# One 512-column matmul for both token parts in the FFN, z and merge-gate products, and one pool of four PSUM banks for products and transposes

## Chip, cores and metric

The kernel runs on one core of one Trainium2 chip. The metric is the device time of one execution in microseconds, as the median of several runs. TensorE is called PE, VectorE DVE, ScalarE ACT, GpSimd POOL, and SyncE, which issues the loads, SP.

## The reference

The input is 256 tokens of width 1024, in fp32. A first block runs four branches on one normalised input and merges them through gates. A second block follows, two layers deep, in which each layer is an FFN, a mixer (MLA in layer 0, NSA in layer 1) and another FFN. Cut to what the change touches:

```python
# first block
h = _rmsnorm(x, norm_pre)
(dn_qkv, dn_z, dn_b, dn_a, gm_uv, gm_z, sw_q, sw_k, sw_v, sw_z,
 xm_q, xm_z, gate_logits) = _split_cols(h @ w_in)
y_a = _deltanet_branch(dn_qkv, dn_z, dn_b, dn_a, ...)   # convolution, L2 norms, chunked delta rule
y_b = _spatial_gating_branch(gm_uv, gm_z, ...)
y_c = _sliding_window_branch(sw_q, sw_k, sw_v, sw_z, sinks)   # attention * silu(z)
y_m = _memory_branch(xm_q, xm_z, mem_kv)                      # attention * silu(z)
proj = einsum("btnc,ncd->btnd", stack([y_a, y_b, y_c, y_m]), w_up)
merged = sum(sigmoid(gate_logits) * proj, axis=2)
x = x + _rmsnorm(merged @ w_out, norm_post)
# second block, for i in (0, 1)
h = h + 0.5 * swiglu(rmsnorm(h, ffn_norm_a[i]), ...)
h = h + (mla_mixer if i == 0 else nsa_mixer)(rmsnorm(h, mix_norm[i]), ...)
h = h + 0.5 * swiglu(rmsnorm(h, ffn_norm_b[i]), ...)
def swiglu(x, w_gate, w_up, w_down):                # hidden width 2816
    return (silu(x @ w_gate) * (x @ w_up)) @ w_down
```

## The kernel before

**Numbers in two parts.** A large product is computed in three matmuls. Weights and activations are each split into a high part, which is the value cast to fp32r, and a low part, which is the remainder. `mm3` (L226 to L232) adds high x high (L227), then the two mixed products (L229 and L231), into one PSUM region. The weights stream in: `unit` (L192) loads up to 1 MB into `raw` (two buffers, SP's queue), ACT casts it to `wh` in two halves (L210), and DVE subtracts to get `wl` (L211), into a ring of four buffers. `transposes` (L328) turns activations on PE, with ACT writing the high part (L356, `xTh`) and DVE the low one (L357, `xTl`).

**Two forms of product.** In `Product` (L240) and `ts` the activations are stationary and 512 weight columns move. In `ws` (L289) a 128x128 block of weights is stationary and the 256 tokens move. One call of `mm3` in `ws` is thus three matmuls of 256 columns, called a triple here. Two row blocks of 256 columns share a 512-column bank, and an evacuation function given by the caller reads the full bank. `ws` is used for z of two branches (`z_ws`, L505), the convolution inputs (`convolve`), two query products of the first block, the merge gates (L1010), the up-projections of the merge, the queries of NSA, and gate and up of every FFN chunk but the first (`hidden`, L1080). `silu2` (L404) is a tanh on ACT (L413) and a multiply on DVE (L414), both from the bank.

**Banks.** PSUM has eight banks. `acc` is a pool of two (L111), `tr`, for transposes, another of two (L114). The other four go to the mixer of the moment (`mm`, `po` and so on) or to the four accumulators `d` of an FFN's down product.

**What sets the order.** The program is written as a stream of large products, with small work dripped into it: after each matmul `drip` takes the next entry of `pending` (a transpose, or a pause) or the next step of a generator in `beside` (deltanet, sliding attention, memory attention). The framework then reorders instructions within each engine by readiness and priority. A tile of a pool is given out in the order in which the program asks for it. So an instruction that needs a new tile of one tag can't be moved ahead of an earlier request of the same tag that is still waiting, while requests of two tags are free of each other.

**Places named below.** First, the deltanet start: `convolve` evacuates a product to `xpad` (L580), runs four taps (ACT, then DVE L586), silu, squares (L597), and `norms` sums the squares with one-column matmuls into a `tr` bank (L603), before the scores of deltanet (L689) and its levels (L721, L730). Second, the tail of sliding attention: scores (L894), softmax on DVE and ACT, transposes of the probabilities `pr` (L335), copies `pT` on DVE (L450), values (L925). Third, the ends of MLA and NSA: the output product (`AddOut`, banks `mm`, `wo`) is added to `res` (L1162), `Normed` squares it on ACT (L312), POOL makes 1/rms (L317, L318), DVE scales (L384, `xn`), PE transposes, and the next FFN begins with `first_hidden`, whose first half of tokens has been transposed earlier.

Of the kernel before, what the change touches and what calls it, by code (L numbers as in the profile page):

```python
# [10 lines left out]
F32 = mybir.dt.float32  # L11
# [6 lines left out]
P = 128  # L18
# [75 lines left out]
def two_blocks_kernel(ctx: ExitStack, tc: tile.TileContext, a, cst_dram, cst2_dram, out):  # L94
# [14 lines left out]
            DEBUG.append("dbg_" + name)  # L109

    def acc():  # L111
        return psum.tile([P, 512], F32, name="acc", bufs=2)

    def tr():  # L114
        return psum.tile([P, 512], F32, name="tr", bufs=2)

    def mixer_banks(stack, *tags):

# [3 lines left out]
    class Turns:  # L122


        def __init__(self, first, second):
            self.banks, self.n = [first, second], 0
# [10 lines left out]
    def drip():  # L137
        for _ in range(pace[0]):
            step()
# [86 lines left out]
    def mm3(ps, ah, al, bh, bl, start, stop):  # L226
# [4 lines left out]
        pe.matmul(ps, al, bh, start=False, stop=stop)  # L231
        drip()  # L232

    def block(x, k, t):

        nb = x[0][0].shape[1]
        h, l = x[k // nb]
        return h[:, k % nb, t * P:(t + 1) * P], l[:, k % nb, t * P:(t + 1) * P]
# [50 lines left out]
    def ws(x, nk, W, r0, c0, n, evac):  # L289

        w = 512 if nk <= 4 else 256
        for j0 in range(0, n, w):
            h, l = unit(W, r0, nk, c0 + j0, w)
            for j1 in range(0, w, 256):
                pv = acc().rearrange("p (j t) -> p j t", j=2)
                for j in range(2):
                    js = slice(j1 + j * P, j1 + (j + 1) * P)
                    for k in range(nk):
                        xh, xl = (v[:, k % v.shape[1], :] for v in x[k // x[0][0].shape[1]])
                        mm3(pv[:, j, :], h[:, k, js], l[:, k, js], xh, xl, k == 0, k == nk - 1)  # L300
                evac((j0 + j1) // P, 2, pv)

    def rstd(ss, eps, n=1):
        r = small.tile([P, n], F32, name=f"rstd{n}")
        gp.tensor_scalar(r, ss, eps, None, op0=OP.add)
        gp.tensor_tensor(r, r, nhalf[:, :n], op=OP.pow)
        return r
# [53 lines left out]
            flush()  # L361

    def xpair():
        h = per.tile([P, 8, T], F32R, name="xTh", bufs=1)
        l = per.tile([P, 8, T], F32R, name="xTl", bufs=1)
        return [(h, l)]

    def ypair():
        h = per.tile([P, 4, T], F32R, name="yTh", bufs=2)
# [34 lines left out]
    def silu2(dst, ps, ph):  # L404

        th = ph.tile([P, 512], F32, name="th", bufs=2)
        n = 1
        for s in ps.shape[1:]:
            n *= s
        thv = th[:, :n]  # L410
        if len(ps.shape) == 3:
            thv = thv.rearrange("p (a b) -> p a b", a=ps.shape[1])
        sc.activation(thv, ps, AF.Tanh, scale=0.5)  # L413
        ve.scalar_tensor_tensor(dst, thv, 1.0, ps, op0=OP.add, op1=OP.mult)  # L414
# [54 lines left out]
    def first(nxt):  # L469
# [36 lines left out]
        def z_ws(name, c0):  # L506

            z = ph.tile([P, 4, T], F32, name="y_" + name)
            y[name] = z
            ws(xT, 8, w_in, 0, c0, 512, lambda j0, w, pv: silu2(z[:, j0:j0 + w, :], pv, ph))  # L510


        bl = ph.tile([P, 2, 8], F32)
# [482 lines left out]
        for at, (br, name) in enumerate([(1, "b"), (2, "c"), (0, "a"), (3, "m")]):  # L996
            if name == "c":
                finish(sliding)
            if name == "m":
                finish(memory)  # L1000
            yT = [ypair()]
            for t in range(2):
                if name in "ab":
                    split_T(y[name][:, t, :], 4, yT, t)
                else:
                    ks_ = slice(2 * t, 2 * t + 2)
                    split(y[name][:, ks_, :], [v[:, ks_, :] for v in yT[0]])
            for n in range(2):
                gate = pg.tile([P, 4, T], F32, name="gate", bufs=1)
                ws(xT, 8, w_in, 0, 5896 + br * D + n * 512, 512,  # L1010
                   lambda j0, w, pv, gate=gate: sc.activation(gate[:, j0:j0 + w, :], pv, AF.Tanh, scale=0.5))
                if at == 3:
                    moT.append(ypair())

                def ev(j0, w, pv, n=n, gate=gate, at=at):
                    g, m = gate[:, j0:j0 + w, :], merged[:, 4 * n + j0:4 * n + j0 + w, :]
                    if at == 0:
                        ve.scalar_tensor_tensor(m, g, 1.0, pv, op0=OP.add, op1=OP.mult)
                    else:
                        ve.scalar_tensor_tensor(g, g, 1.0, pv, op0=OP.add, op1=OP.mult)  # L1020
                        ve.tensor_add(m, m, g)
                    if at == 3:
                        split(m, [v[:, j0:j0 + w, :] for v in moT[n]])

                ws(yT, 4, a["w_up"][0, br], 0, n * 512, 512, ev)
# [27 lines left out]
    def ffn(i, which, xn, nxt, aside=None):  # L1053
        pace[0] = 1
        wg, wu, wd = (a[f"ffn_{which}_w_{s}_2"][i] for s in ("gate", "up", "down"))
        nxt.load()
        fx = ExitStack()
        pf = fx.enter_context(tc.tile_pool(name=f"ffn{which}{i}", bufs=2))
        pd = fx.enter_context(tc.tile_pool(name="down", bufs=1, space=bass.MemoryType.PSUM))
        dacc = {(t, m): pd.tile([P, 512], F32, name=f"d{t}{m}") for t in range(2) for m in range(2)}  # L1060
        xT = xn.x
        chunks = [(0, 512), (512, 512), (1024, 512), (1536, 512), (2048, 256), (2304, 512)]

        def first_hidden(c0, n):

            sg = {}

            def ev_g(t, g, p):
                sg[t] = pf.tile([P, 512], F32, name="sg", bufs=4)
                silu2(sg[t], p, pf)  # L1070

            def ev_u(t, g, p):
                ve.tensor_mul(sg[t], sg[t], p)

            pg = Product(xT, 8, wg, 0, c0, n, ev_g)
            pu = Product(xT, 8, wu, 0, c0, n, ev_u)
            in_turns([(pg, 0), (pg, 1), (pu, 0), (pu, 1)], lead=4)
            hT = [ypair()]
            for t in range(2):
                split_T(sg[t], n // P, hT, t, wait=LAG_HIDDEN if t == 0 else 0)  # L1080
            return hT

        def hidden(c0, n):

            hT = ypair()
            for j0 in range(0, n, 256):
                sg = pf.tile([P, 2, T], F32, name="sg", bufs=4)

                def ev_u(j, w, p, js=slice(j0 // P, j0 // P + 2), sg=sg):
                    ve.tensor_mul(sg, sg, p)  # L1090
                    sc.copy(hT[0][:, js, :], sg)
                    ve.tensor_sub(hT[1][:, js, :], sg, f32(hT[0][:, js, :]))

                ws(xT, 8, wg, 0, c0 + j0, 256, lambda j, w, p, sg=sg: silu2(sg, p, pf))
                ws(xT, 8, wu, 0, c0 + j0, 256, ev_u)
            return [hT]

        def down_units(c0, n):
            nk = n // P
            if nk == 4:  # L1100
                return {m: units(wd, c0, nk, m * 512, 512)[0] for m in range(2)}
            both, = units(wd, c0, nk, 0, D)
            return {m: [(h[:, halves[m]], l[:, halves[m]]) for h, l in both] for m in range(2)}

        def down(us, hT, t, m, first, last):
            nk = len(us[m])
            for k, (h, l) in enumerate(us[m]):
                mm3(dacc[t, m], *block(hT, k, t), h, l, first and k == 0, last and k == nk - 1)

        def add_down(t, m):  # L1110
            ve.scalar_tensor_tensor(res[:, t, halves[m]], dacc[t, m], 0.25, res[:, t, halves[m]],
                                    op0=OP.mult, op1=OP.add)

        prev = None
        for c, (c0, n) in enumerate(chunks):
            hT = hidden(c0, n) if c else first_hidden(c0, n)
            if prev is not None and c < len(chunks) - 1:
                us = down_units(*prev[:2])
                for m in range(2):
                    for t in range(2):  # L1120
                        down(us, prev[2], t, m, c == 1, False)
            elif prev is not None:
                held = (down_units(*prev[:2]), prev[2])
                for m in range(2):
                    down(*held, 0, m, False, False)
            prev = (c0, n, hT)
            if c == 1 and aside:
                aside()
        us = down_units(*prev[:2])
        for m in range(2):  # L1130
            down(us, prev[2], 0, m, False, True)
            add_down(0, m)
        nxt(0)
        for m in range(2):
            down(*held, 1, m, False, False)
        for m in range(2):
            down(us, prev[2], 1, m, False, True)
            add_down(1, m)
        nxt(1)
        fx.close()  # L1140
# [542 lines left out]
```

## Time and profile before

| | us |
|---|---|
| median of 3 runs | 1436.03 (1435.72 to 1440.63) |
| profiled execution, its own time | 1434.2 |
| its span in the profile | 1432.4 |
| PE busy | 1408.2 (98%) |
| DVE busy | 873.9 (61%) |
| ACT busy | 686.5 (48%) |
| POOL busy | 44.3 (3%) |

The profile is one execution. Its own time is 1.8 us longer than its span. "Busy" of PE is modelled, since matmuls overlap: the row of a matmul gives its start and a duration that reaches into the next one. What a matmul takes of PE's time is read from the distance between two starts. Every row gives line, engine, operation, output and input tile, shape, and in square brackets the idle time of that engine just before and what ended it.

### The profile page before, as it was taken

To read this page: it belongs to the slowest core of one execution; us is meant where nothing else is said; L and a number is where in the kernel's file an instruction comes from. 1 tells how busy PE (TensorE), PEld (TensorE's weight loads), DVE (VectorE), ACT (ScalarE), POOL (GpSimd) and SP (SyncE) were. 2 spreads that over 40 slices of the span, in tenths; PEclk is the share of its full clock that TensorE was granted. 3 is DMA by queue.
4 is the path that set the end of the run, shared out by engine and by line. 5 is a ranking of instruction groups with operands and counts; after the bars stand their busy time and mean duration, and the time that the engine had idled before them with its cause. 6 is when DMAs were issued, how large, how long until landed. Compare 5 with 4: busy or idle time off the path is not lost.

```text
span 1432.4 us, 23501 instructions
## 1 busy us (share of the span) xinstructions
PE 1408.2 (98%) x9712; PEld 1278.7 (89%) x9712; DVE 873.9 (61%) x1443; ACT 686.5 (48%) x1149; POOL 44.3 (3%) x87
## 2 busy tenths in 40 slices
PE   7999999999999999999999999999999999999998
PEld 7998989999979999887799998999898976799997
DVE  6878575565576555668565546655555676665544
ACT  6646454443354433466453435443435376554432
POOL 1002000000010000110000000000000000000000
PEclk9999999999999999999999999999999999999999
DMA  7425634555546655433567655565665620465551
GB/s 260 143 89 177 220 107 144 177 177 177 177 157 215 198 180 180 161 119 121 167 208 257 212 177 183 184 206 177 201 205 182 168 60 30 133 201 185 195 185 59
DMA packets 172543, 241.90 MB, mean 169 GB/s; under 512 B 5263, under 2 KB 121748, under 8 KB 172308
## 3 DMA queue, kind: packets, MB, share of 16 engines
q1 hardware_dynamic: 172436, 240.40, 52.3%
q8 instruction: 76, 1.25, 0.3%
q14 instruction: 31, 0.25, 0.1%
HBM read 239.31 MB, written 4.22 MB: 170 GB/s over the span
## 4 chain that ended last, share of the span: by engine, by line
PE 91%; DMA 3%; DVE 2%; ACT 2%; POOL 1%; issue 1%; SPq 0%; POOLq 0%; ACTq 0%
PE acc L231 20%; PE acc L227 20%; PE acc L229 20%; PE d L227 5%; PE d L229 5%; PE d L231 5%; PE tr L335 4%; DMA raw<-in_nsa_w_in_dram 1%; DVE wl L211 1%; ACT wh L210 1%; PE wo L1512 1%; PE mm L1512 1%; PE po L730 1%; PE po L721 1%; DMA raw<-in_ffn_b_w_up_dram 1%
## 5 line engine op out<-in xcount | busy, mean ns | idle before, releaser
L211 DVE TENSOR_TENSOR wl<-raw,wh 128x1024 fp32r<-128x1024 f32 (+5 forms) x434 | 512.5, 1198 | 330.3 <-ACT wh L210 329.6
L210 ACT CAST wh<-raw 128x1024 fp32r<-128x1024 f32 (+5 forms) x434 | 436.1, 1028 | 527.3 <-PE acc L229 278.8
L227 PE MATMUL acc<-xTh,wh 128*128 128x256 f32 x1696 | 483.3, 285 | 0.0
L229 PE MATMUL acc<-xTl,wh 128*128 128x256 f32 x1696 | 483.1, 285 | 0.0
L231 PE MATMUL acc<-xTh,wl 128*128 128x256 f32 x1696 | 482.8, 285 | 0.0
L227 PEld LDWEIGHTS acc<-xTh,wh 128*128 128x128 f32 x1696 | 325.1, 192 | 2.2 <-PE d L231 0.6
L229 PEld LDWEIGHTS acc<-xTl,wh 128*128 128x128 f32 x1696 | 325.2, 192 | 1.4 <-issue 0.3
L231 PEld LDWEIGHTS acc<-xTh,wl 128*128 128x128 f32 x1696 | 325.2, 192 | 0.7 <-issue 0.5
L227 PE MATMUL d<-wh,yTh 128*128 128x512 f32 x352 | 137.7, 391 | 0.0
L229 PE MATMUL d<-wl,yTh 128*128 128x512 f32 x352 | 137.7, 391 | 0.0
L231 PE MATMUL d<-wh,yTl 128*128 128x512 f32 x352 | 137.7, 391 | 0.0
L227 PE MATMUL acc<-wh,xTh 128*128 128x512 f32 (+4 forms) x256 | 97.6, 382 | 0.5 <-ACT xTh L356 0.5
L231 PE MATMUL acc<-wh,xTl 128*128 128x512 f32 (+4 forms) x256 | 96.2, 378 | 0.2 <-DVE xTl L357 0.2
L229 PE MATMUL acc<-wl,xTh 128*128 128x512 f32 (+4 forms) x256 | 96.2, 376 | 0.0
L231 PEld LDWEIGHTS d<-wh,yTl 128*128 128x128 f32 x352 | 66.1, 188 | 14.3
L227 PEld LDWEIGHTS d<-wh,yTh 128*128 128x128 f32 x352 | 66.2, 188 | 13.4
L229 PEld LDWEIGHTS d<-wl,yTh 128*128 128x128 f32 x352 | 66.2, 188 | 13.1
L1090 DVE TENSOR_TENSOR sg<-sg,acc 128x512 f32<-128x512 f32 x36 | 24.7, 687 | 53.3 <-PE acc L231 53.3
L231 PEld LDWEIGHTS acc<-wh,xTl 128*128 128x128 f32 x256 | 48.6, 190 | 8.9 <-DVE xTl L357 0.9
L227 PEld LDWEIGHTS acc<-wh,xTh 128*128 128x128 f32 x256 | 48.8, 191 | 8.7 <-ACT xTh L356 1.2
L229 PEld LDWEIGHTS acc<-wl,xTh 128*128 128x128 f32 x256 | 48.9, 191 | 7.5
L231 PE MATMUL acc<-yTh,wl 128*128 128x256 f32 x160 | 45.5, 284 | 0.0
(442 smaller groups left out, 1753.2 us busy)
## 6 DMA issues: line engine op xcount, KB each, us to landing
raw<-in_w_in_dram SPq DMA_DIRECT2D x37, 1024.0 KB, 5.2
raw<-in_ffn_a_w_gate_dram SPq DMA_DIRECT2D x22, 1024.0 KB, 5.3
raw<-in_ffn_a_w_up_dram SPq DMA_DIRECT2D x22, 1024.0 KB, 5.4
raw<-in_ffn_a_w_down_dram SPq DMA_DIRECT2D x22, 1024.0 KB, 5.0
raw<-in_ffn_b_w_gate_dram SPq DMA_DIRECT2D x22, 1024.0 KB, 5.4
raw<-in_ffn_b_w_up_dram SPq DMA_DIRECT2D x22, 1024.0 KB, 5.3
raw<-in_ffn_b_w_down_dram SPq DMA_DIRECT2D x22, 1024.0 KB, 5.1
raw<-in_w_up_dram SPq DMA_DIRECT2D x8, 1024.0 KB, 5.0
```

The costliest lines, as they stand in the source:

```text
L210: sc.copy(h[:, c], raw[:, c])
L211: ve.tensor_sub(l[:, c], raw[:, c], f32(h[:, c]))
L227: pe.matmul(ps, ah, bh, start=start, stop=False)
L229: pe.matmul(ps, ah, bl, start=False, stop=False)
L231: pe.matmul(ps, al, bh, start=False, stop=stop)
L335: pe.transpose(box[0][:m, b * P:(b + 1) * P], src(b), ident)
L721: pe.matmul(pv[:, h], O[:, h, :], dv[:, h], start=True, stop=True)
L730: pe.matmul(p[:, h * 64:(h + 1) * 64], Em[:, h, :], Vs[t][:, h, :], start=True, stop=True)
L1090: ve.tensor_mul(sg, sg, p)
L1512: pe.matmul(s[:, i, :], qT[half(h), h // 2, tsl], kT[br][half(h), h // 4, 0:w], start=True, stop=True)
```

## The change

A class `Pair` holds high and low part of the activations in one tile of shape 128 x 8 x 2 x 256, so that both parts of one k are adjacent. A new function `ws2` does the product of `ws` with two matmuls for each k: one of 512 columns with the high weights (both parts at once, into both halves of a bank), one of 256 columns with the low weights (into the first half). Each 128-row block has a bank of its own. The evacuation is an ACT copy of the second half to SBUF and a DVE add of the first half, and then the caller's function reads SBUF. `ws2` takes the place of `ws` for the two z products, the merge gates, and gate and up of the FFN chunks but the first. `acc` gets four banks, and `tr` becomes another name of `acc`.

```diff
     def acc():
-        return psum.tile([P, 512], F32, name="acc", bufs=2)
-
-    def tr():
-        return psum.tile([P, 512], F32, name="tr", bufs=2)
+        return psum.tile([P, 512], F32, name="acc", bufs=4)
+
+    tr = acc
...
+    class Pair:
+        def __init__(self, t):
+            self.t = t
+            self.parts = (t[:, :, 0, :], t[:, :, 1, :])
...
+        def both(self, k):
+            return self.t[:, k]
...
+    def ws2(x, nk, W, r0, c0, n, into, evac=None, scale=None):
+        w = 512 if nk <= 4 else 256
+        for j0 in range(0, n, w):
+            h, l = unit(W, r0, nk, c0 + j0, w)
+            for j1 in range(0, w, 256):
+                b = (j0 + j1) // P
+                dst = into(b)
+                for j in range(2):
+                    js = slice(j1 + j * P, j1 + (j + 1) * P)
+                    ps = acc()
+                    for k in range(nk):
+                        pair = x[k // x[0][0].shape[1]]
+                        kk = k % pair[0].shape[1]
+                        for part in ("hl" if k == 0 else "lh"):
+                            if part == "h":
+                                pe.matmul(ps, h[:, k, js], pair.both(kk), start=k == 0, stop=k == nk - 1)
+                                drip()
+                            else:
+                                pe.matmul(ps[:, :T], l[:, k, js], pair[0][:, kk, :], start=False, stop=False)
+                            drip()
+                    d = dst[:, j, :]
+                    if scale is None:
+                        sc.copy(d, ps[:, T:])
+                        ve.tensor_add(d, d, ps[:, :T])
...
+                if evac:
+                    evac(b, 2, dst)
...
     def xpair():
-        h = per.tile([P, 8, T], F32R, name="xTh", bufs=1)
-        l = per.tile([P, 8, T], F32R, name="xTl", bufs=1)
-        return [(h, l)]
+        return [Pair(per.tile([P, 8, 2, T], F32R, name="xT", bufs=1))]
...
-            ws(xT, 8, w_in, 0, c0, 512, lambda j0, w, pv: silu2(z[:, j0:j0 + w, :], pv, ph))
+            ws2(xT, 8, w_in, 0, c0, 512, lambda j0: z[:, j0:j0 + 2, :], lambda j0, w, pv: silu2(pv, pv, ph))
...
-                ws(xT, 8, w_in, 0, 5896 + br * D + n * 512, 512,
-                   lambda j0, w, pv, gate=gate: sc.activation(gate[:, j0:j0 + w, :], pv, AF.Tanh, scale=0.5))
+                ws2(xT, 8, w_in, 0, 5896 + br * D + n * 512, 512,
+                    lambda j0, gate=gate: gate[:, j0:j0 + 2, :],
+                    lambda j0, w, pv: sc.activation(pv, pv, AF.Tanh, scale=0.5))
...
-                ws(xT, 8, wg, 0, c0 + j0, 256, lambda j, w, p, sg=sg: silu2(sg, p, pf))
-                ws(xT, 8, wu, 0, c0 + j0, 256, ev_u)
+                ws2(xT, 8, wg, 0, c0 + j0, 256, lambda j, sg=sg: sg, lambda j, w, p: silu2(p, p, pf))
+                ws2(xT, 8, wu, 0, c0 + j0, 256, lambda j: pf.tile([P, 2, T], F32, name="up", bufs=2), ev_u)
```

The order of instructions changes beyond the products. In the rows below a line number of the changed kernel differs from that of the kernel before: L226, L228, L230 are `mm3`, L336 and L339 are `ws2`, L383 is the transpose, L940 the scores, L943 their mask, L971 the values of sliding attention.

PE, tail of sliding attention, before, from the first values product of the stretch; `acc<-xTh,wh` and its two fellows are products of the large stream.

```order
L925 MATMUL po<-pT,vs 64x128 x4
L227 MATMUL acc<-xTh,wh 128x256
L229 MATMUL acc<-xTl,wh 128x256
...
L231 MATMUL acc<-xTh,wl 128x256
L227 MATMUL acc<-xTh,wh 128x256
L894 MATMUL mm<-ksT,qs 128x512
L897 LDWEIGHTS identb
L897 MATMUL mm<-maskb,identb 128x256
L897 LDWEIGHTS identb
L897 MATMUL mm<-maskb,identb 128x256
L335 MATMUL tr<-cst,pr 128x128 x4
```

PE at the same place in the changed kernel.

```order
L971 MATMUL po<-pT,vs 64x128 x4
L940 MATMUL mm<-ksT,qs 128x512
L943 LDWEIGHTS identb
L943 MATMUL mm<-maskb,identb 128x256
L943 LDWEIGHTS identb
L943 MATMUL mm<-maskb,identb 128x256
L940 MATMUL mm<-ksT,qs 128x512
L383 MATMUL acc<-cst,pr 128x128 x4
L943 LDWEIGHTS identb
L943 MATMUL mm<-maskb,identb 128x256
L383 MATMUL acc<-cst,pr 128x128 x4
```

Up to the last values product of the stretch 65 matmuls of the large stream stand between these steps before (13 of them between the first two), and 9 now, all behind the last transposes; the other 56 follow later.

PE, end of NSA, before; the `acc` rows are the next FFN's `first_hidden`, 17 matmuls ahead of the first transpose.

```order
L227 MATMUL acc<-wh,xTh 128x512
L229 MATMUL acc<-wl,xTh 128x512
L335 MATMUL tr<-cst,xn 128x128 x4
L231 MATMUL acc<-wh,xTl 128x512
L335 MATMUL tr<-cst,xn 128x128 x4
L227 MATMUL acc<-wh,xTh 128x512
```

PE at the same place in the changed kernel; `wo` is the mixer's output product.

```order
L230 MATMUL wo_11459<-wh,yTl 128x512
L383 MATMUL acc<-cst,xn 128x128 x8
L226 MATMUL acc<-wh,xT 128x512
L228 MATMUL acc<-wl,xT 128x512
L230 MATMUL acc<-wh,xT 128x512
```

All of `first_hidden` now stands behind the transposes. At the end of MLA it is alike: 18 matmuls ahead of the transposes before, none now.

PE, deltanet start, before; `acc` rows are the last convolution product, `Em` holds squares.

```order
L227 MATMUL acc<-xTh,wh 128x256
L229 MATMUL acc<-xTl,wh 128x256
L689 MATMUL mm<-qk 128x256 x2
L603 MATMUL tr<-cst,Em 128x1 x4
L231 MATMUL acc<-xTh,wl 128x256
L227 MATMUL acc<-xTh,wh 128x256
...
L227 MATMUL acc<-xTh,wh 128x256
L689 MATMUL mm<-qk 128x256 x2
L603 MATMUL tr<-cst,Em 128x1 x4
```

PE at the same place in the changed kernel (L735 are the scores, L649 the sums of squares).

```order
L230 MATMUL acc<-xT,wl 128x256
L735 MATMUL mm<-qk 128x256 x2
L649 MATMUL acc<-cst,Em 128x1 x4
L735 MATMUL mm<-qk 128x256
L649 MATMUL acc<-cst,Em 128x1 x4
L226 MATMUL acc<-xT,wh 128x256
```

Before the second sum of squares 54 matmuls (18 triples) of the last convolution product fewer stand now, and some of them drip between the matmuls of deltanet's levels later.

## Rows read from the trace of the kernel before

**Rows 1.** The page: busy time of PE, and the clock in 40 slices.

```profile
PE 1408.2 (98%) x9712; PEld 1278.7 (89%) x9712; DVE 873.9 (61%) x1443; ACT 686.5 (48%) x1149; POOL 44.3 (3%) x87
PEclk9999999999999999999999999999999999999999
```

**Rows 2.** Timeline, PE: start, duration, line; from 512-column to 256-column matmuls.

```profile
420.09 0.39 PE L227 MATMUL acc<-wh,xTh 128*128 128x512 f32 x1
...
420.77 0.39 PE L227 MATMUL acc<-wh,xTh 128*128 128x512 f32 x1
...
430.06 0.39 PE L231 MATMUL acc<-wh,xTl 128*128 128x512 f32 x1
430.29 0.28 PE L227 MATMUL acc<-xTh,wh 128*128 128x256 f32 x1
...
431.00 0.28 PE L227 MATMUL acc<-xTh,wh 128*128 128x256 f32 x1
```

**Rows 3.** Groups by form: count, busy us, mean ns, idle before them.

```profile
L211 DVE TENSOR_TENSOR wl<-raw,wh 128x1024 fp32r<-128x1024 f32 x406 | 489.7, 1222 | 322.6 <-ACT wh L210 322.1
L210 ACT CAST wh<-raw 128x1024 fp32r<-128x1024 f32 x406 | 416.3, 1047 | 512.2 <-PE acc L229 275.5 <-PE d L231 100.9 <-PE acc L231 29.1
L732 DVE TENSOR_TENSOR Dm<-Dm,po 128x256 f32<-128x256 f32 x12 | 5.1, 421 | 7.1 <-PE po L730 7.1
L724 ACT COPY Vc<-po 128x256 f32<-128x256 f32 x12 | 4.5, 371 | 4.3 <-PE po L721 4.3
```

**Rows 4.** Busy us (instructions) by engine, clock, DMA share, GB/s: FFN, deltanet start, sliding tail.

```profile
468.00:504.00 36.00, 36.00 (x260) 34.11 (x259) 18.75 (x19) 14.01 (x16) 0.00 (x0) 1.00 0.56 176
54.30:63.56 9.26, 9.17 (x71) 8.61 (x69) 8.02 (x16) 7.14 (x12) 0.10 (x1) 1.00 0.64 222
197.37:212.73 15.36, 15.36 (x130) 12.64 (x129) 13.01 (x34) 9.19 (x26) 0.00 (x0) 1.00 0.23 70
```

**Rows 5.** Timeline, end of MLA: PE.

```profile
698.05 0.40 PE L227 MATMUL acc<-wh,xTh 128*128 128x512 f32 x1
...
701.94 0.39 PE L231 MATMUL acc<-wh,xTl 128*128 128x512 f32 x1
703.19 1.29 PE L335 MATMUL tr<-cst,xn 128*128 128x128 f32 x8 [0.86 <-DVE xn L384]
```

**Rows 6.** Timeline, end of NSA: PE.

```profile
1236.88 0.39 PE L227 MATMUL acc<-wh,xTh 128*128 128x512 f32 x1
...
1242.19 0.63 PE L335 MATMUL tr<-cst,xn 128*128 128x128 f32 x4 [1.30 <-DVE xn L384]
```

**Rows 7.** Timeline, deltanet start, all engines.

```profile
54.30 0.59 ACT L580 COPY xpad<-acc 128x512 f32<-128x512 f32 x1 [0.21 <-PE acc L231]
...
58.06 2.45 DVE L586 SCALAR_TENSOR_TENSOR qk<-xpad,cwT,qk 128x256 f32<-128x256 f32 x6
...
63.56 0.61 PE L603 MATMUL tr<-cst,Em 128*128 128x1 f32 x4
```

**Rows 8.** Timeline, PE, at the start of the program.

```profile
8.38 1.97 PE L335 MATMUL tr<-cst,xn 128*128 128x128 f32 x8 [8.38 <-DVE xn L384]
...
12.35 0.41 PE L227 MATMUL acc<-wh,xTh 128*128 128x256 f32 x1
...
13.65 0.37 PE L227 MATMUL acc<-wh,xTh 128*128 128x256 f32 x1
...
14.09 0.28 PE L227 MATMUL acc<-wh,xTh 128*128 128x264 f32 x1
...
14.80 0.28 PE L227 MATMUL acc<-wh,xTh 128*128 128x264 f32 x1
```

**Rows 9.** Busy by engine and clock (third number from the end), end of the span.

```profile
1425.70:1432.40 6.70, 0.04 (x1) 0.00 (x0) 1.87 (x3) 1.45 (x3) 0.86 (x2) 0.85 0.21 78
...
1428.00:1430.00 2.00, 0.00 (x0) 0.00 (x0) 0.48 (x1) 0.72 (x1) 0.32 (x1) 1.00 0.15 55
1430.00:1432.40 2.40, 0.00 (x0) 0.00 (x0) 0.00 (x0) 0.00 (x0) 0.00 (x0) 0.57 0.46 172
```

More of the change, by code (lines that the diff above doesn't have):

```diff
@@ L232, in mm3, with __getitem__, __iter__ @@
         drip()
+    class Pair:
+        def __init__(self, t):
+            self.t = t
+            self.parts = (t[:, :, 0, :], t[:, :, 1, :])
+        def __getitem__(self, i):
+            return self.parts[i]
+        def __iter__(self):
+            return iter(self.parts)
+        def both(self, k):
+            return self.t[:, k]
     def block(x, k, t):
@@ L301, in ws @@
                 evac((j0 + j1) // P, 2, pv)
+    def ws2(x, nk, W, r0, c0, n, into, evac=None, scale=None):
[22 more added lines that the diff above has]
+                        ve.tensor_add(d, d, ps[:, :T])
+                    else:
+                        sc.activation(d, ps[:, T:], AF.Copy, scale=scale)
+                        ve.scalar_tensor_tensor(d, ps[:, :T], scale, d, op0=OP.mult, op1=OP.add)
+                if evac:
+                    evac(b, 2, dst)
     def rstd(ss, eps, n=1):
```

## Prediction

> **What bounds the kernel now.** I read the engine totals first, then PE's timeline, then the stretches that the order of instructions changes. In the totals [rows 1] the reader is to see that PE is busy 98% of the span, with the clock full in all slices, so time is won or lost only where PE's work shrinks or where PE stands still. In the FFN [rows 4] (first row) PE is busy for all 36 us of a 36 us stretch, ACT for 14.01 and DVE for 18.75; both have room there. In two other stretches, deltanet's start and the sliding tail [rows 4] (second and third row), DVE is busy 8.02 of 9.26 us and 13.01 of 15.36 us: there PE is full only because products of the large stream are dripped between the steps of a DVE-bound chain. The measured execution took 1434.2 us, 1.8 under the median of 1436.03; I add all differences up against the former and give the result on the scale of the latter.
>
> **What the wide matmul saves.** In PE's timeline [rows 2] three 512-column matmuls take 0.68 us from start to start (420.09 to 420.77), 226.7 ns each; the one after which a 256-column matmul follows takes 0.23 (430.06 to 430.29), so the mix costs nothing extra; six of 256 columns take 0.71 (430.29 to 431.00), 118 to 120 ns each, and over longer stretches I read 120. Doubling the columns adds 106.7 ns, so each matmul carries 13.3 ns that don't grow with columns. A triple of 256 takes 360 ns, a pair of 512 and 256 takes 346.7: the columns are the same 768, one fixed part goes. Counted from the code: z 2 x 4 blocks x 8 k = 64, merge gates 4 x 8 x 8 = 256, FFN 4 x 18 blocks x 2 x 8 = 1152, in sum 1472. 1472 x 13.3 ns = **19.6 us less** (15.4 of it in the FFNs). The nearest doubt is the stationary load: 512-column matmuls with a load each run at this pitch already [rows 2], so I see no bound there.
>
> The Trainium skill (TensorE: Matmul & The Clock Gate, section "Wait — 56ns, not 53.3ns?") gives a fixed cost of about 2.5 ns per matmul at full clock; by that the saving would be an estimated 3.7 us. The rows above show 13.3 ns for this fp32r stream, and no page is needed for the sum.
>
> **What the evacuations add.** Each of the 184 blocks gets an ACT copy and a DVE add of 128x256; the nearest rows [rows 3] are 371 ns (L724) and 421 ns (L732), so 68 us of ACT and 77 of DVE in all, less for later steps that read SBUF. In an FFN a weight unit of 1 MB holds two blocks: 0.74 us of ACT and 0.84 of DVE in about 5.6 us of PE. ACT goes from 39% to some 52%, DVE from 52% to some 67%. In [rows 3] the casts wait for PE, not PE for casts: the ring is full and three units ahead. I take nothing for it; if the cover failed at the last block of a last chunk, four times some 0.4 us, that is at most 1.6 us. SP's order of loads stays, and POOL's work too.
>
> **What the shared pool moves.** A transposition now asks for a tile of the pool that the products use. A product written after it may not be hoisted ahead of it while it waits. That is where the order shows PE losing cover; the waits themselves are as old as the kernel.
>
> *Ends of MLA and NSA.* The norm chain (DVE add, ACT squares, POOL, DVE scale) lasts from the last output matmul to the first transpose: 698.05 to 703.19, 5.1 us [rows 5]; 1236.88 to 1242.19, 5.3 us [rows 6]. Before, 18 and 17 matmuls of `first_hidden` stand inside it; now all stand behind. The chain has its own engines and doesn't get shorter. 18 x 0.2267 = 4.1 us and 17 x 0.2267 = 3.9 us, **8.0 us more**. Bounds: 6 if the chain shortens by a weight cast that gives way, 9 if the transposes come later.
>
> *Deltanet start.* The chain from the evacuation of the last query product at 54.30, over the taps at 58.06, to the sum of squares at 63.56 lasts 9.3 us [rows 7]; 54 product matmuls (6.5 us at 120 ns) that lay inside or ahead of it come later. Bounds: 6.5 us if it stays as long, and 5.3 if all of DVE's slack of 1.24 us [rows 4] (second row) is taken out. I take 5.5, near the lower end because casts queued on ACT and DVE come later as well. Two of the first levels lose their fillers too, some 12 matmuls of 512 columns, most of which the later levels don't need: I take 1.0, between 0 and 2.7 (12 x 0.2267). **6.5 us more.**
>
> *Sliding tail.* The stretch from the first values product to the end of the last is 15.4 us long [rows 4] (third row). 56 of the 65 product matmuls in it come later, 6.7 us of PE. DVE is busy 13.01 us in the stretch [rows 4] (third row); without pacing by products, the chain can shorten by DVE's idle 2.35 us. So 6.7 - 2.4 = **4.3 us more**, between 2 (a pair of weight subtractions leaves the chain also, 2 x 1.22 [rows 3]) and 6.7.
>
> *The rest.* In memory attention a few triples stand later: I take 1 us, from 0 to 2. MLA's attention and NSA's late queries are reordered without a clear direction; 1 us, from -2 to 4. Two spare banks for products bring nothing that I can see: PE's time is full wherever the product stream runs alone [rows 4] (first row).
>
> Sum: -19.6 + 8.0 + 6.5 + 4.3 + 2 = **+1.2 us**.
>
> **The clock.** PE would stand idle for over 5 us at the ends of MLA and NSA. At the end of the span PE has stopped at 1425.7; the record shows the full clock until 1430 and 0.57 as the mean of the last 2.4 us [rows 9], that is, a fall to half, from 2.4 to 1.2 GHz, between 4.3 and some 4.7 us after the stop. So an idle stretch of 5.1 to 5.3 us lies just at the point. What a slow phase costs: at the start of the program six matmuls take 1.30 us (12.35 to 13.65) and six alike later 0.71 (14.09 to 14.80) [rows 8]; the slow phase lasts from PE's first work at 8.38 to 13.65, some 5.3 us, so a return loses about 5.3 x (1 - 0.71/1.30) = 2.4 us. I put one of two falls into the forecast: +1.2 + 2.4 = +3.6, less a little for a transposition phase that is slow anyway: about **+3 us, 1439**.
>
> The same page of the Trainium skill (section "Why this matters for your kernels") warns against idle gaps of PE between bursts, since the array then returns to its low clock. By that rule both ends fall; the row at the end of the span agrees with it in kind.
>
> **Rivals.**
> *Fillers were not worth their time (faster).* If the chains shorten when PE no longer paces them, and ACT's and DVE's weight work steps back, the four terms halve: -19.6 + 10.4 = -9.2 us, 1427. For it: ACT has 2 us of slack in the deltanet start [rows 4]. Against it: DVE is the engine at its limit and has less slack than that, and the norm chain runs through POOL and ACT with nothing to give up.
> *Idle PE, slow PE (slower).* Both ends fall to the half clock, the deltanet start and the sliding tail do also since PE there works in crumbs: four phases at 2.4 us instead of one, +1.2 + 9.6 = +10.8, and the later copies on ACT push the softmax chain: 1447 to 1450. [...] Against it: in those two stretches single matmuls come every 1 to 3 us.
> *The saving isn't there (slower).* If the fixed part belongs to the bank or the accumulation region rather than to the instruction, alternating 512 and 256 columns in one bank saves 0 to 4 us: 1454 to 1460. The switch row at 430.06 speaks against it. The change then does not do what it says.
>
> **How the numbers follow.** Chances: forecast (the sum, with none, one or two falls: 1434 to 1443) 0.52; faster rival, with the pool terms halved, 0.20; slow clock 0.22; no saving 0.06. Half a per cent, 7.2 us, is about what a measurement of this kernel can tell from no change: below 1428.8 is faster, above 1443.2 slower. The faster case lies around 1427, just beyond, so faster has 0.18 and 0.02 goes to the middle: faster 0.18, same 0.54, slower 0.28. The range reaches over the faster rival and the slow clock: 1424 to 1449; outside lie the last rival and a further shortening of the chains.
>
> **What would show it.** Starts of pairs in an FFN 346.7 ns apart, and FFN stretches without idle PE; each 16-pair unit 0.21 us shorter. At the ends of MLA and NSA PE idle for about 5 us, ended by `xn`, with the transposes first; pitches of the matmuls behind them at 0.22 us per 256 columns or 0.12 tell whether the clock fell. PE idle of some 5 us between the two sums of squares, and 4 to 5 in the sliding tail. Wrong would be: copies of L343 that come so late that PE waits for a bank in the FFN; or pairs at 360 ns; or the chains above shorter by half.

## Result

The changed kernel takes 1470.35 us (1465.65 to 1473.51), the kernel before 1436.82 in the same comparison: a ratio of 1.0234 (1.0217 to 1.0250), 33.5 us slower. The forecast was 1439 with a range of 1424 to 1449. The profiled execution is the fastest of the four, 1465.65 us, with a span of 1463.9.

The page of the changed kernel: busy us and share by engine, PE's share in tenths and the granted clock in tenths, over 40 slices. Beside it [rows 1].

```profile
PE 1414.1 (97%) x8240; PEld 1211.5 (83%) x8240; DVE 940.9 (64%) x1627; ACT 748.4 (51%) x1333; POOL 45.8 (3%) x87
...
PE   7799999999999999999899999999999999899998
...
PEclk9889999999999999999999999999999999999999
```

1472 matmuls are gone and PE is nonetheless busy 6 us longer. The granted clock, at nine tenths or more in every slice before, is below 0.9 in the second and third slice. The span is 31.5 us longer than the profiled one before: 25.6 us of that is more idle PE (1463.9 - 1414.1 against 1432.4 - 1408.2), 5.9 us more busy PE.

Waits of PE, changed kernel, the longest of the view: total, number of times, longest.

```profile
PE acc L383 <- DVE xn L430: 20.8, 5, 9.0
PE mm L735 <- DVE qk L460: 6.0, 2, 3.2
PE acc L383 <- DVE pr L920: 2.5, 3, 2.1
PE acc L649 <- ACT Dm L643: 2.1, 1, 2.1
PE acc L383 <- DVE lat L1243: 1.9, 1, 1.9
PE po L767 <- DVE Dm L747: 1.5, 1, 1.5
```

PE waits at the places that the prediction named: for `xn` at the ends of MLA and NSA, in deltanet's start and its levels (`Dm`), in the sliding tail (`pr`). The wait for MLA's latents (`lat`) is not in the prediction; it is 0.9 us before. (9.0 us of the first row are the start of the program, 8.4 before.)

Timeline, PE, the ends of MLA and of NSA in the changed kernel; they answer to [rows 5, 6].

```profile
724.25 0.40 PE L230 MATMUL wo<-wh,oTl 128*128 128x512 f32 x1
729.53 1.96 PE L383 MATMUL acc<-cst,xn 128*128 128x128 f32 x8 [4.89 <-DVE xn L430]
731.14 0.78 PE L226 MATMUL acc<-wh,xT 128*128 128x512 f32 x1
```

```profile
1264.98 0.39 PE L230 MATMUL wo<-wh,yTl 128*128 128x512 f32 x1
1270.47 1.94 PE L383 MATMUL acc<-cst,xn 128*128 128x128 f32 x8 [5.10 <-DVE xn L430]
```

Timeline, PE, deltanet's start: the longest waits there [rows 7].

```profile
62.32 1.13 PE L735 MATMUL mm<-qk 128*128 128x256 f32 x4 [2.76 <-DVE qk L460]
...
68.22 1.22 PE L735 MATMUL mm<-qk 128*128 128x256 f32 x2 [3.23 <-DVE qk L460]
```

Busy us of PE, PEld, DVE, ACT, POOL (instructions), then granted clock, DMA share, GB/s, in stretches of the changed kernel; of before [rows 4].

```profile
60.00:66.00 6.00, 2.60 (x12) 2.06 (x12) 5.23 (x13) 5.35 (x9) 0.21 (x2) 0.83 0.40 150
66.00:72.00 6.00, 3.79 (x15) 3.56 (x16) 4.60 (x7) 0.87 (x2) 0.00 (x0) 0.50 0.58 186
72.00:78.00 6.00, 6.00 (x35) 5.64 (x35) 3.48 (x10) 0.00 (x0) 0.00 (x0) 0.82 0.44 164
84.00:90.00 6.00, 6.00 (x33) 6.00 (x32) 3.41 (x9) 1.32 (x3) 0.00 (x0) 0.54 0.01 3
...
729.50:733.00 3.50, 3.47 (x13) 3.09 (x14) 3.50 (x5) 1.42 (x3) 0.00 (x0) 0.51 0.78 249
...
1270.00:1276.00 6.00, 5.53 (x18) 4.76 (x19) 4.45 (x6) 1.63 (x3) 0.00 (x0) 0.53 0.95 322
```

In deltanet's start PE is idle for more than half of 60 to 66, then runs at half the clock (1.2 instead of 2.4 GHz) until past 72, and again from 84. The third row of [rows 4] has its counterpart too: in the sliding tail PE waits up to 2.1 us at a time (the `pr` row of the waits).

What the clock takes can be estimated: PE's busy time times one minus the granted clock, summed over stretches of 1 us through the whole span, is 17.9 us in this execution, and nothing in the kernel before until PE's work is over. These 17.9 us lie in eight slow phases: three in deltanet (they begin at 46.9, 64.0 and 84.5 us and take 1.7, 3.5 and 3.4 us), one in the sliding tail (227.8; 1.7), one behind the wait for MLA's latents (637.4; 1.7), one at the end of MLA (729.6; 1.6), one inside NSA (1176.7; 1.7), one at the end of NSA (1268.9; 2.6). By stages, read from the starts of certain matmuls (us):

| | before | changed | difference grows by |
|---|---|---|---|
| start of the spatial branch | 130.0 | 149.6 | 19.6 |
| first down matmul of the first FFN | 454.2 | 477.5 | 3.7 |
| last down matmul of the first FFN | 595.3 | 616.2 | -2.4 |
| first down matmul after MLA | 745.9 | 777.2 | 10.4 |
| last one before NSA | 1076.3 | 1102.6 | -5.0 |
| first one after NSA | 1285.0 | 1318.9 | 7.6 |
| last matmul | 1425.3 | 1456.8 | -2.4 |

The stretches with an FFN gain; those with deltanet, sliding attention, MLA or NSA, where transposes wait for other engines, lose.

### The profile page after: what moved, and what is told of

It reads as the page before. It is cut to its first block, busy times and chain, and to the rows that moved or that the text cites. A ratio compares the mean times of both kernels' runs of the same rounds, so it can differ in the third digit from the quotient of the medians.

```text
span 1463.9 us, 20857 instructions
## 1 busy us (share of the span) xinstructions
PE 1414.1 (97%) x8240; PEld 1211.5 (83%) x8240; DVE 940.9 (64%) x1627; ACT 748.4 (51%) x1333; POOL 45.8 (3%) x87
## 4 chain that ended last, share of the span: by engine, by line
PE 89%; DVE 4%; ACT 2%; DMA 2%; issue 1%; POOL 1%; SPq 0%; POOLq 0%; ACTq 0%; DVEq 0%
PE acc L336 23%; PE acc L339 12%; PE acc L226 7%; PE acc L228 7%; PE acc L230 7%; PE d L230 5%; PE d L226 5%; PE d L228 5%; PE acc L383 5%; DVE wl L210 1%; PE po L776 1%; PE po L767 1%; ACT wh L209 1%; DMA raw<-in_ffn_b_w_up_dram 1%; PE wo L1559 1%
## 5 line engine op out<-in xcount | busy, mean ns | idle before, releaser
L336 PE MATMUL acc<-xT,wh 128*128 128x512 f32 x1472 | 509.4, 397 | 0.0
L339 PE MATMUL acc<-xT,wl 128*128 128x256 f32 x1472 | 382.4, 280 | 0.0
L336 PEld LDWEIGHTS acc<-xT,wh 128*128 128x128 f32 x1472 | 265.3, 188 | 51.0 <-issue 0.6
L339 PEld LDWEIGHTS acc<-xT,wl 128*128 128x128 f32 x1472 | 277.4, 188 | 15.6
L230 PE MATMUL d<-wh,yTl 128*128 128x512 f32 x352 | 138.0, 392 | 0.0
L226 PE MATMUL d<-wh,yTh 128*128 128x512 f32 x352 | 137.6, 391 | 0.0
L228 PE MATMUL d<-wl,yTh 128*128 128x512 f32 x352 | 137.5, 391 | 0.0
L226 PE MATMUL acc<-wh,xT 128*128 128x512 f32 (+4 forms) x256 | 98.9, 386 | 0.6 <-ACT xT L404 0.6
L228 PE MATMUL acc<-wl,xT 128*128 128x512 f32 (+4 forms) x256 | 97.7, 382 | 0.0
L230 PE MATMUL acc<-wh,xT 128*128 128x512 f32 (+4 forms) x256 | 97.0, 381 | 0.0
L230 PEld LDWEIGHTS d<-wh,yTl 128*128 128x128 f32 x352 | 66.1, 188 | 14.9 <-DVE yTl L1139 0.8
L228 PEld LDWEIGHTS d<-wl,yTh 128*128 128x128 f32 x352 | 66.1, 188 | 14.1
L226 PEld LDWEIGHTS d<-wh,yTh 128*128 128x128 f32 x352 | 66.1, 188 | 13.1
L343 ACT COPY sg<-acc 128x256 f32<-128x256 f32 x72 | 27.0, 375 | 88.9 <-PE acc L336 88.6
L226 PE MATMUL acc<-xT,wh 128*128 128x256 f32 x224 | 68.1, 304 | 0.0
L228 PE MATMUL acc<-xT,wh 128*128 128x256 f32 x224 | 67.7, 302 | 0.0
L230 PE MATMUL acc<-xT,wl 128*128 128x256 f32 x224 | 66.5, 297 | 0.0
L344 DVE TENSOR_TENSOR sg<-sg,acc 128x256 f32<-128x256 f32 x72 | 29.9, 416 | 52.8 <-ACT sg L343 52.8
L226 PEld LDWEIGHTS acc<-wh,xT 128*128 128x128 f32 x256 | 49.9, 195 | 9.2 <-ACT xT L404 1.0
```

What stands on the lines that cost most here:

```text
L226: pe.matmul(ps, ah, bh, start=start, stop=False)
L228: pe.matmul(ps, ah, bl, start=False, stop=False)
L336: pe.matmul(ps, h[:, k, js], pair.both(kk), start=k == 0, stop=k == nk - 1)
L339: pe.matmul(ps[:, :T], l[:, k, js], pair[0][:, kk, :], start=False, stop=False)
L343: sc.copy(d, ps[:, T:])
L344: ve.tensor_add(d, d, ps[:, :T])
```

## Experiments

Theory A: the one pool loses the time, since products can no longer be hoisted ahead of waiting transposes. Theory B: the wide product itself does, through its bank for each block and its copies and adds.

**Two pools again.** The changed kernel with

```diff
-        return psum.tile([P, 512], F32, name="acc", bufs=4)
-
-    tr = acc
+        return psum.tile([P, 512], F32, name="acc", bufs=2)
+
+    def tr():
+        return psum.tile([P, 512], F32, name="tr", bufs=2)
```

> The changed kernel with two pools again: two banks acc for products, two banks tr for transposes; the wide products stay. Theory A (the one pool loses the time, since products can no longer be hoisted ahead of waiting transposes): the fillers are back at the deltanet start, the sliding tail and the ends of MLA and NSA, the granted clock stays full, and the pairs save about 10.5 ns each as they do in the changed kernel's FFNs, 1472 x 10.5 = 15.5 us: 1418 to 1426 us. Theory B (the wide product itself loses it: a bank for each block, copies on ACT and adds on DVE in front of casts and of the mixers' chains): still slower than before, 1445 to 1470 us, and more with two banks than with four.

Measured: 1421.02 us (1420.04 to 1421.86), a ratio to before of 0.9895 (0.9879 to 0.9912). The wide product alone gains 14.4 us. The clock from its page, then deltanet's start and an FFN by stretch:

```profile
PEclk9999999999999999999999999999999999999999
...
60.00:66.00 6.00, 5.90 (x44) 5.35 (x43) 4.86 (x13) 4.53 (x7) 0.10 (x1) 1.00 0.21 80
66.00:72.00 6.00, 6.00 (x50) 5.86 (x48) 5.54 (x13) 0.34 (x1) 0.00 (x0) 1.00 0.01 3
...
468.00:504.00 36.00, 36.00 (x194) 30.89 (x193) 23.27 (x29) 18.74 (x28) 0.00 (x0) 1.00 0.56 189
```

Theory B is out: the copies and adds raise DVE and ACT in the FFN from 18.75 and 14.01 [rows 4] to 23.27 and 18.74 of 36 us, and PE stays full.

**The pool alone.** The kernel before with

```diff
-        return psum.tile([P, 512], F32, name="acc", bufs=2)
-
-    def tr():
-        return psum.tile([P, 512], F32, name="tr", bufs=2)
+        return psum.tile([P, 512], F32, name="acc", bufs=4)
+
+    tr = acc
```

> The kernel before with one edit: one pool of four banks for products and transposes; products of 256 columns as before. Theory A: all of the loss without the gain, 1436 + 33 + 15 = about 1484 us (1474 to 1492), with the clock falling at the same places. Theory B: as before or a little better through more banks, 1430 to 1440 us.

Measured: 1483.33 us (1479.32 to 1494.06), a ratio of 1.0343 (1.0290 to 1.0395), 47.9 us slower. The two parts add up: -14.4 + 47.9 = 33.5, and 33.5 was measured for both together. Theory A holds: the whole loss comes from making one pool of the two.

**Three banks and one.** `acc` with three banks, `tr` with one, else as the first run.

> The changed kernel with two pools, three banks acc and one bank tr. Theory A: order as in the kernel before, but one bank for transposes makes each group of four transposes wait for the evacuation of the one before (0.6 to 1.3 us each, at the norms and the attention's transposes): 1420 to 1440 us. Theory B: 1445 to 1470 us, better than with two banks acc.

Measured: 1422.51 us (1421.79 to 1422.81), ratio 0.9905 (0.9889 to 0.9921). A single bank for all transposes, with a third one for products, costs 1.5 us against two and two. What the transposes need is a pool of their own, not more banks. This is the base for the four runs further below.

**All four banks for the FFN's blocks, two pools.**

```diff
+    four = Turns(tr, acc)
...
-                    ps = acc()
+                    ps = ps_of()
...
-                ws2(xT, 8, wg, 0, c0 + j0, 256, lambda j, sg=sg: sg, lambda j, w, p: silu2(p, p, pf))
+                ws2(xT, 8, wg, 0, c0 + j0, 256, lambda j, sg=sg: sg, lambda j, w, p: silu2(p, p, pf), ps_of=four)
```

(the same for `up`).

> The changed kernel with two pools of two banks, and in the FFN the blocks of the wide products take banks of tr and acc in turns. Theory A: equal to the kernel with two pools within 3 us, or up to 5 us better if two banks make PE wait there for evacuations: 1415 to 1426 us. Theory B: 1445 us or more, since the copies and adds are all still there.

Measured: 1420.51 us (1420.31 to 1420.67), ratio 0.9892 (0.9876 to 0.9907). The medians differ by 0.5 us from the run with two banks each, which is less than the runs of that kernel lie apart (1.8 us), so a gain is not shown. PE's wait for a bank in the run with two banks each is no larger than this either: 1.5 us of idle time before the wide matmuls, 1.1 of it for an add of L345:

```profile
L337 PE MATMUL acc<-xT,wh 128*128 128x512 f32 x1472 | 509.9, 397 | 1.5 <-DVE sg L345 1.1
```

**One place at a time.** From the kernel with three banks and one, single groups of transposes were put on the products' pool. First the sums of squares in `norms`:

```diff
-                    box.append(tr())
+                    box.append(acc())
                 pe.matmul(box[0][:, i:i + 1], sq[:, i * P:(i + 1) * P], C("ones", 0, 1), start=True, stop=True)
```

> The changed kernel with three banks acc and one bank tr (1422.5 us), and one place put back on the products' pool: the banks into which norms sums the squares of q and k. Theory A1 (the deltanet start is lost by these sums standing ahead of the convolution products, with the clock's fall behind the idle time): most of the 19 us that the changed kernel loses up to the spatial branch come back, 1434 to 1443 us. Theory A2 (the loss is in the levels' transposes, which no filler can pass): 1422 to 1428 us.

Measured: 1435.84 us (1433.04 to 1442.90), ratio 1.0008 (0.9992 to 1.0025): 13.3 us more than the base. PE's waits (three were 2.15, 2.76 and 3.23 us, the last two below) and the clock behind them:

```profile
61.17 1.76 PE L736 MATMUL mm<-qk 128*128 128x256 f32 x4 [2.76 <-DVE qk L461]
...
67.65 1.22 PE L736 MATMUL mm<-qk 128*128 128x256 f32 x2 [3.23 <-DVE qk L461]
```

```profile
55.00:61.00 6.00, 3.41 (x29) 3.20 (x27) 6.00 (x10) 3.27 (x7) 0.10 (x1) 1.00 0.61 203
61.00:67.00 6.00, 3.25 (x12) 2.82 (x12) 4.63 (x13) 3.81 (x5) 0.10 (x1) 0.54 0.04 16
67.00:73.00 6.00, 5.35 (x23) 5.12 (x24) 3.03 (x4) 0.63 (x1) 0.00 (x0) 0.50 0.82 273
73.00:79.00 6.00, 6.00 (x35) 5.49 (x35) 4.51 (x12) 0.00 (x0) 0.00 (x0) 0.82 0.20 76
```

The clock falls after an idle stretch of 2.8 us and stays at half for nearly 14 us, through one more wait (3.23 us) and some 7 us of work without a pause. By busy time times one minus clock that is 5.2 us; the other 8 us are PE standing still, three times. This is theory A1.

Then the transposes of deltanet's levels as well (`of=acc` in both calls of `transposes` there).

> As the run before, with the transposes of deltanet's levels on the products' pool as well. Theory A1: little more than the sums alone, at most 4 us. Theory A2: 1436 to 1443 us, and the step from the run before is over 8 us.

Measured: 1442.28 us (1439.66 to 1449.28), ratio 1.0054 (1.0030 to 1.0077): 6.4 us more, neither A1's 4 nor A2's 8. The clock's loss grows from 5.2 to 8.6 us: two phases up to 75 take 5.2 us together, and a further one from 84 to 92 takes 3.4. It stands behind a new wait of 1.5 us, for `Dm` in the levels. Where the remaining 1.5 us lie is not shown.

The transposes of the attentions' probabilities:

```diff
-                pending.extend(transposes(lambda b: p[:, b * P:(b + 1) * P], nb, after))
+                pending.extend(transposes(lambda b: p[:, b * P:(b + 1) * P], nb, after, of=acc))
```

> Three banks acc and one bank tr (1422.5 us), with only the transposes of the attentions' probabilities (sliding, memory, MLA, NSA) on the products' pool. By the prediction's terms 4.3 for the sliding tail, 1 for memory, 1 for the rest: 1428 to 1430 us. By the stages of the changed kernel, 6 us in the first block, some 3 to 7 in MLA and 0 to 3 in NSA: 1431 to 1439 us.

Measured: 1437.19 us (1436.28 to 1444.17), ratio 1.0014 (0.9998 to 1.0030): 14.7 us, against 6.3 in the prediction. By stages, from the two profiles, 10.3 of it up to the first down matmul, 2.7 in MLA, 1.3 in NSA. In the sliding tail:

```profile
210.84 1.09 PE L384 MATMUL acc<-cst,pr 128*128 128x128 f32 x4 [2.71 <-ACT pr L957]
...
208.00:214.00 6.00, 2.51 (x17) 1.67 (x14) 3.49 (x13) 2.02 (x9) 0.00 (x0) 0.71 0.54 175
214.00:220.00 6.00, 6.00 (x41) 5.53 (x41) 1.38 (x2) 0.00 (x0) 0.00 (x0) 0.72 0.00 0
```

PE is idle for 3.5 of 6 us and the clock falls here too, which takes 2.8 us by the same sum.

The transposes of the normalised activations (`split_T` from `norm_T` with `of=acc`):

> Three banks acc and one bank tr (1422.5 us), with only the transposes of the normalised activations on the products' pool. By the prediction: 8.0 us for the fillers at the ends of MLA and NSA, plus the clock: 1430.5 us if it doesn't fall, 1433 to 1436 us if it falls at both ends as in the changed kernel.

Measured: 1432.69 us (1431.56 to 1433.78), ratio 0.9978 (0.9968 to 0.9987): 10.2 us, with two slow phases, at the ends of MLA and NSA, that take 4.6 us. One of them, and the idle PE ahead of it:

```profile
694.00:700.00 6.00, 1.11 (x6) 0.62 (x5) 4.36 (x7) 5.22 (x8) 1.97 (x3) 1.00 0.92 290
700.00:706.00 6.00, 6.00 (x24) 4.86 (x23) 3.84 (x5) 1.18 (x2) 0.00 (x0) 0.72 0.97 255
```

The four places together give 13.3 + 6.4 + 14.7 + 10.2 = 44.6 of the 47.8 us that lie between the base and the changed kernel. No run was made for the rest, 3 us. It can be the transposes not tried (MLA's and NSA's latents, keys and queries), or the places are not quite additive. For the latents the changed kernel's profile speaks: the wait for `lat` is 1.1 us longer there than before, and a slow phase of 1.7 us follows it. The clock's share in the four places is 8.6 + 2.8 + 4.6 = 16.0 us, in their profiled executions.

**Other order at the ends, same pool.** The changed kernel with

```diff
-        finish(work)
+        while work in beside:
+            step()
```

in `mla` and `nsa`, so that the pending transposes are asked for during `first_hidden`.

> The changed kernel, one pool of four banks, with one edit at the ends of MLA and NSA: finish no longer empties the list of pending work, so the transposes of the last norm are asked for during first_hidden and not ahead of it. If the order at the ends alone costs what the run with only these transposes on the products' pool showed (10.2 us), and the two stalls of before (1.0 and 1.5 us) go as well: 1456 to 1461 us. If the prediction's 8.0 us hold and the clock has no part in it: 1460 to 1463 us. If the ends are covered otherwise: 1468 to 1472 us.

Measured: 1457.89 us (1456.23 to 1459.00), ratio 1.0151 (1.0136 to 1.0166), 12.5 us less than the changed kernel. From the last down matmul before MLA to the first after it 152.8 us instead of 161.0, around NSA 207.3 instead of 216.3; 1.7 us of each difference is a slow phase ahead of the edit (at 637 and 1176) that this profile doesn't have. At the ends it is not the shared banks that cost here but the place at which the program asks for them.

This run's profile shows something else. Its instructions up to the end of MLA are those of the changed kernel, yet it reaches the spatial branch at 158.2 us and not at 149.6:

```profile
84.00:90.00 6.00, 5.32 (x34) 5.32 (x35) 4.52 (x11) 2.27 (x4) 0.00 (x0) 0.71 0.01 3
90.00:96.00 6.00, 6.00 (x30) 6.00 (x30) 1.87 (x3) 1.23 (x3) 0.00 (x0) 0.50 0.00 0
96.00:102.00 6.00, 6.00 (x31) 5.94 (x30) 3.94 (x6) 2.07 (x4) 0.00 (x0) 0.50 0.27 80
102.00:108.00 6.00, 6.00 (x29) 6.00 (x29) 1.44 (x3) 0.37 (x1) 0.00 (x0) 0.50 0.27 95
108.00:114.00 6.00, 6.00 (x45) 6.00 (x45) 1.80 (x3) 1.92 (x4) 0.00 (x0) 0.80 0.01 3
```

The same stretch of the changed kernel's own profile:

```profile
96.00:102.00 6.00, 6.00 (x56) 6.00 (x55) 3.61 (x6) 2.55 (x6) 0.00 (x0) 1.00 0.53 175
102.00:108.00 6.00, 6.00 (x56) 6.00 (x55) 2.23 (x4) 1.80 (x5) 0.00 (x0) 1.00 0.01 3
```

The instructions and their order are the same, but the slow phase lasts from 86 to 111 here and from 84 to 92 there, and takes 11.9 against 3.4 us. This can explain why the changed kernel's four executions lie 8 us apart, while those of the kernels with two pools lie within 2. For three of the four only time and mean clock are on record; they are the longer ones, with a mean clock of 0.978 to 0.981 against 0.985, which fits but doesn't show the place.

**Keeping PE awake at the ends.** The changed kernel with 20 unused matmuls in the wait:

```diff
-        finish(work)
+        while work in beside:
+            step()
+        ps, xh = mm1(), add_out.oT[0][0]
+        for _ in range(20):
+            pe.matmul(ps, xh[:, 0, 0:P], xh[:, 0:2, :].rearrange("p a t -> p (a t)"), start=True, stop=True)
+        flush()
```

> The changed kernel with 20 matmuls of 512 columns, whose result nobody reads, at the ends of MLA and of NSA, in the time in which PE waits for the norm (20 x 0.227 = 4.5 us). They take no waiting away. If the clock's fall behind these two idle stretches costs what the trace's granted clock says (PE busy at half speed for some 7 us in all, 3.5 us lost): 1465.5 to 1468 us, and no clock below 0.95 in the 12 us behind them. If idle time alone makes the loss: 1469 to 1472 us.

Measured: 1469.15 us (1462.49 to 1470.51), ratio 1.0217 (1.0190 to 1.0245). The total lies in the range that was given for idle time alone, but it decides nothing: the executions lie 8 us apart, and the profiled one has the long slow phase from 86 to 110. The trace tells more. At the end of MLA the unused matmuls fill the wait, and the clock stays:

```profile
738.60 1.32 PE L383 MATMUL acc<-cst,xn 128*128 128x128 f32 x8
...
732.00:737.00 5.00, 5.00 (x24) 4.08 (x23) 3.68 (x4) 3.24 (x6) 0.59 (x1) 1.00 0.72 233
737.00:742.00 5.00, 4.86 (x25) 3.66 (x24) 4.21 (x5) 3.18 (x4) 1.21 (x3) 1.00 0.78 270
```

The eight transposes take 1.07 us up to the next matmul, where the changed kernel took 1.61 (729.53 to 731.14). Around MLA the time falls from 161.0 to 159.4 us, around NSA from 216.3 to 212.3, 1.7 of which is a slow phase at 1176, ahead of the edit, that this profile doesn't have. So the clock is worth 1.6 and some 2.3 us at the two ends, near the 1.6 and 2.6 that busy time times one minus clock gives; of the 10.2 us at these ends the idle time is the larger part.

**Both findings in one kernel.** Two pools, the FFN's blocks in turns, and the other order at the ends.

> The kernel with the wide products, two pools of two banks with the FFN's blocks taking banks of both in turns (1420.5 us), and the late emptying of the pending list at the ends of MLA and NSA. If the stalls of 1.0 and 1.5 us there go: 1416.5 to 1419 us. If the transposes then come too late for the second half of tokens: 1420 to 1424 us.

Measured: 1417.94 us (1417.45 to 1418.43), ratio 0.9873 (0.9859 to 0.9888): 18.2 us faster than the kernel before. The waits for `xn` at the ends of MLA and NSA, which the kernel before has too, are gone. The list of its longest waits begins:

```profile
PE tr L384 <- DVE xn L431: 11.0, 4, 8.6
PE po L704 <- DVE Ob L812: 0.9, 1, 0.9
```

(8.6 us is the start of the program, the remaining 2.4 other norms.)

## Why the prediction was wrong

**The wide matmul** was right in kind and over-sized. It gains 14.4 us and not 19.6. The pair takes 350 ns and not 346.7, as the FFN of the changed kernel shows:

```profile
501.07 0.40 PE L336 MATMUL acc<-xT,wh 128*128 128x512 f32 x1
501.31 0.28 PE L339 MATMUL acc<-xT,wl 128*128 128x256 f32 x1
501.42 0.40 PE L336 MATMUL acc<-xT,wh 128*128 128x512 f32 x1
```

From the wide start to the narrow one 0.24 us, and 0.11 to the next; the medians over all such steps are 233 and 117 ns, against 227 and 120 of before. The single switch row at 430.06 in [rows 2] was a switch of another kind and didn't carry the claim "costs nothing extra". 14.4 us over 1472 pairs is 9.8 ns each. The rival "no saving", and with it the 2.5 ns per matmul of the Trainium skill's page "TensorE: Matmul & The Clock Gate" (section "Wait — 56ns, not 53.3ns?"), is out for this stream by the run with two pools.

**The evacuations** cost nothing in the changed kernel, as said: its page shows 0.0 us of idle time before the wide matmuls.

**What the pool moves**: all four places were found from the order, and all lose. The terms' sum was 20.8 us without the clock. The four runs give 44.6 with it and 28.6 without its 16.0; as this takes the clock of single executions from medians, the figures without it are rough. The changed kernel's page gives a second reading, all from one execution: 25.6 us more idle PE. So the idle time was forecast some 5 us too low, and most of the miss lies elsewhere.
- The ends: 8.0 us were forecast for the fillers. Idle time before `xn` grew from 0.86 and 1.30 us [rows 5, 6] to 4.89 and 5.10, that is 7.8. Right.
- Deltanet's start: 6.5 us were forecast, 19.7 measured (13.3 and 6.4), 11.1 of it without the clock. The step that failed here: I took the wait between two sums of squares as one stretch with DVE's slack as its only play. PE stands still at three places there, for 2.15, 2.76 and 3.23 us; the first, at the sums of the keys, was not in my sum.
- The attentions: 6.3 us were forecast (4.3, 1 and 1), 14.7 measured, 11.9 without the clock. In the first block, where sliding and memory attention stand, 5.3 were forecast and 10.3 measured, 7.5 without the clock. The bound of 6.7 us for the sliding tail assumed that only the moved products are lost.

**The clock** is the step that failed most: 2.4 us were forecast, 16 to 18 measured. The price of a phase was about right, 2.4 us against a mean of 2.2 in the changed kernel's profile. The number was wrong: one phase went into the sum, and there were eight. I expected a fall only behind an idle stretch like that at the end of the span, where PE had stopped for over 4.3 us [rows 9], so only the two ends counted; in the changed kernel waits of 2.76, 2.15, 1.93 and 1.55 us stood before falls. And the length of a phase, taken from the start of the program (5.3 us, [rows 8]), is not that of the other places: it is 3.4 to 10.2 us in that profile, nearly 14 in the run with only the sums of squares on the pool, and 24 in one execution with the levels. The rival "idle PE, slow PE" had the mechanism and four of the places, at which six of the eight phases lie, and gave 1447 to 1450 at a chance of 0.22. "PE there works in crumbs" was its condition; "single matmuls come every 1 to 3 us" was named as evidence against it, and did not keep the clock up. Waits don't explain a phase's length, though: in the longest, from 86 to 111, the profile shows no wait of PE.

The page of the Trainium skill named above (section "Why this matters for your kernels") warns of idle gaps between bursts, as cited in the prediction. The runs agree: with the gap at the end of MLA filled the granted clock stays at 1.00, without, it falls to 0.51.

## What to carry to other kernels

Tiles that are given out in program order tie together everything that asks for the same tag: a transpose that waits for a slow chain then holds back all later products. Where a scheduler fills waits with independent work, that work needs a pool of its own, even of a single bank (1.5 us here, against 48 for the shared one). When an order shows PE losing its cover, count each wait that comes to light, price it as idle time, and allow for a slow phase behind it, whose length nothing in an undisturbed trace shows.

## What the runs showed of the hardware

- A slow phase of TensorE can last long after the wait ahead of it. With PE modelled as busy in every stretch, the granted clock stayed at 0.50 from 90 to 108 us in one execution, and was back at 1.00 from 96 in another execution of the same instructions. The spatial branch, next after it, started 8.6 us later in the former.
- Short idle stretches stood before falls, and the same stretches stood without one. In the changed kernel 2.76, 2.15, 1.93 and 1.55 us came before falls; 2.15 us had none in the run with only the sums of squares on the pool, nor had 1.93 us (the wait for `lat`) in the run with the other order at the ends. At 1176.7 the changed kernel's clock fell although no wait in the 16 us ahead was above 0.44 us. What decides between these is open.

```profile
1170.00:1176.00 6.00, 5.15 (x43) 4.23 (x41) 5.83 (x36) 3.50 (x19) 0.00 (x0) 1.00 0.41 107
1176.00:1182.00 6.00, 6.00 (x39) 5.27 (x40) 2.81 (x22) 4.25 (x17) 0.31 (x1) 0.72 0.35 72
```

- Alternating 512-column and 256-column fp32r matmuls into one bank take 233 and 117 ns (medians in the changed kernel), 350 for the pair, 3 more than the sum of the two alone (227 and 120 in the kernel before).
